# Low query parts and gate rows as 128-row operands padded with zeros, in a two-layer hybrid decoder step

## The chip, the cores and the metric

The kernel runs on one core of a Trainium2 chip. The metric is the device time of one execution in microseconds; the time of a kernel is the median of its runs.

## The reference

One step of a decoder with two trunk layers, for a prompt of 1024 tokens and a sample group of 8 x 4 tokens with 4096 cached ones each. A layer has a combined projection, four gated DeltaNet heads beside four differential attention heads, an output projection, a cross-attention and a gated MLP. What the change touches is the causal attention of the prompt (two 64-wide softmax maps per head) and the decay matrix of the DeltaNet:

```python
def diff_attention(q, k, v, q_pos, k_pos, lam):
    ...
        s = jnp.einsum('bqhd,bkhd->bhqk', qi, k).astype(jnp.float32) * scale
        s = jnp.where(k_pos[None, None, None, :] <= pi[None, None, :, None], s, -jnp.inf)
        p = jax.nn.softmax(s, axis=-1).reshape(B, H, 2, qb, Lk)
        a = p[:, :, 0] - lam * p[:, :, 1]
        return jnp.einsum('bhqk,bkhe->bqhe', a.astype(v.dtype), v)

def gated_delta_rule(q, k, v, g, beta, s0):
    ...
    gc = jnp.cumsum(chunks(g), axis=-1)
    decay = jnp.exp(jnp.where(lower, gc[..., :, None] - gc[..., None, :], -jnp.inf))
    kb = kc * bc[..., None]
    m = jnp.where(strict, jnp.einsum('nbhid,nbhjd->nbhij', kb, kc) * decay, 0.0)
    ...
```

Data are float32. The kernel multiplies at a shorter type with operands cut in two, a high part and a low part (the rest), and adds the products.

## The kernel before

Each layer runs as two interleaved streams: the prompt's (projection, DeltaNet beside attention, output projection, cross-attention, MLP) and the sample group's, which reads the cached keys and values page by page (tiles kn and vn) and is fed in between. A scheduler (the tile framework with its own model of the engines) fixes the order of all instructions on each engine when the program is built; on the chip each engine runs its own list in order and waits for semaphores.

TensorE holds one operand, the weights, which a load (LDWEIGHTS, shown as engine PEld) brings in, and streams the other. All of the TensorE's instructions are recorded at line 219, the helper that passes them on, so they are told apart by their tiles; a row "psA<-akT,aq" is a matmul into the accumulator psA that streams akT over the weights aq. A form 64\*128 means weights of 64 rows and 128 columns.

**Attention of the prompt** (`attn`, entered once a layer, after the projection). Queries and keys lie in DRAM as high and low parts (qksc), 64 dimensions for each of the two maps m of a head. `load` brings the keys of a head, tile akT, of 128 rows: for map 0 the high parts in rows 0 to 63 and the low parts in rows 64 to 127, for map 1 the other way round. `qload` brings the queries of two token tiles (256 tokens), tile aq, in three planes: planes 0 and 1 hold the high part of map 0 and 1 twice, in both halves of the rows, and plane 2 holds the low parts of both maps, map m in rows 64m to 64m+63. `scores` then makes, for a map and up to 512 keys, two matmuls into one accumulator: plane m against all 128 rows of akT (high query with high and low keys), and 64 rows of plane 2 against the 64 rows of akT with the high keys, placed at row 64m by tile_position. On the last piece a bfloat16 matmul of the mask cmn with an identity (identb) follows. DVE takes the maximum (mx), ScalarE the exponential (apr), and `values` transposes and multiplies with aV. There are 4 heads x 8 token tiles x 2 maps in a layer, in one piece of keys for the first four token tiles and two for the rest.

**DeltaNet.** `Gdn.rows` turns the cumulated gates of a chunk of 128 tokens into rows: tile hk, 64 rows, the high part from row 0, the low part from row 32, all else zero (zeroed by POOL). `decay` multiplies hk with the block pattern bma on POOL (tile R, L1170), and makes the exponent with three matmuls: R over weights of ones (oner, 64 rows), the block pattern bmbr over weights hk (64 rows), and the mask cmtb over identb (128 rows). `inputs` runs R over oner once more, alone. The eight chunks pass through `decay` in `gdn_first` (beside the end of the projection) and again in `gdn` (beside attention); the sample group passes once, in `gdn_samples`.

Queries, keys, pages and DeltaNet inputs all go out on SyncE's DMA queue (SP), in its order.

Of the kernel before, what the change touches and what calls it, by code (L numbers as in the profile page):

```python
# [9 lines left out]
F32 = mybir.dt.float32  # L10
F32R = mybir.dt.float32r
# [8 lines left out]
P = 128  # L20
# [165 lines left out]
def build(tc, a, out, depth=2):  # L186
# [12 lines left out]
    BC = (lambda z: z.bitcast(F32)) if XP[0] != '0' else (lambda z: z)  # L199
# [6 lines left out]
    QD = {'0': nc.gpsimd, '1': nc.scalar, '2': nc.sync}[XP[0]]  # L206
# [19 lines left out]
    v_, s_, g_, t_ = Tracked(nc.vector), nc.scalar, nc.gpsimd, Tracked(nc.tensor)  # L226
# [77 lines left out]
    def cload(pool_, key, rows=P, name=None, **kw):  # L304
        o, w = COFF[key]
        tl = pool_.tile([rows, w], F32, name=name or f"c_{key}", **kw)
        nc.sync.dma_start(tl, cst[0:rows, o:o + w])
        return tl
# [10 lines left out]
    ones = cp.tile([P, P], F32, name="ones")  # L319
# [5 lines left out]
    qksc = dp.tile([2, 2, 4, P, NP], F32, name="qksc")  # L325
# [205 lines left out]
    for t in range(9):  # L531
# [6 lines left out]
        for hf in range(2):  # L538
            ps = psA((P, 4, P))
# [6 lines left out]
    for k0 in range(0, KT, 3):  # L546
        m = min(3, KT - k0)
        raw = ip.tile([P, D], F32, tag="xt", bufs=5, name="raw")[:, 0:m * 264].rearrange("p (k c) -> p k c", c=264)
        nc.sync.dma_start(raw, a["w_in"][0][k0 * P:(k0 + m) * P, 2048:2312].rearrange("(k p) c -> p k c", p=P))
        for k in range(m):  # L550
            if (k0 + k) % 2 == 0:
                t = dk.tile([P, 1056], F32R, name="pre", tag="pg", bufs=PGB).rearrange("p (a b c) -> p a b c", a=2, b=2)
            hi, lo = t[:, (k0 + k) % 2, 0], t[:, (k0 + k) % 2, 1]
# [112 lines left out]
    for l in range(depth):  # L666
# [391 lines left out]
        class Gdn:  # L1058


            def __init__(self, gw, nh, nrow, tp, tag):
                self.gw, self.nh, self.nrow = gw, nh, nrow
                self.cm = gw.tile([P, P], BF16, name="cmtb")
                tmp = cload(tp, "cmt" if nh == 4 else "cmts", name="cmtmp", tag=tag, bufs=1)
                v_.tensor_copy(self.cm, tmp)
                self.utm = cload(gw, "ut" if nh == 4 else "uts")
                self.glm = ones if nh == 4 else cload(gw, "blks")
                self.oner = gw.tile([64, P], F32R, name="oner")
                v_.tensor_copy(self.oner, ones[0:64])
                self.bma = cload(gw, f"bma{nh}", rows=64)  # L1070
                tb_ = cload(gw, f"bmb{nh}", rows=64)
                self.bmb = gw.tile([64, nh, P], F32R, name="bmbr")
                v_.tensor_copy(self.bmb, bcast(tb_, 2, P))

            def small(self, nm, sh):
# [77 lines left out]
            def rows(self, f):  # L1153

                nh = self.nh
                tk = self.gw.tile([P, 2 * nh], F32, name="tk", tag="tk", bufs=2)
                g_.tensor_copy(tk[:, 0:nh], f["gc"])
                g_.tensor_copy(tk[:, nh:2 * nh], f["bias"])
                pt = psG()
                t_.transpose(pt[0:2 * nh, 0:P], tk, ident)  # L1160
                hk = self.gw.tile([64, P], F32R, name="hk", tag="hk", bufs=self.nrow)
                g_.memset(hk.bitcast(F32), 0.0)
                s_.copy(hk[0:2 * nh, :], pt[0:2 * nh, 0:P])
                v_.tensor_tensor(hk[32:32 + 2 * nh, :], pt[0:2 * nh, 0:P], hk[0:2 * nh, :].bitcast(F32), op=ALU.subtract)
                return hk

            def decay(self, wk, hk, bufs):
                nh = self.nh
                R = wk.tile([64, nh, P], F32R, name="R", tag="R", bufs=1)
                g_.tensor_tensor(R, bcast(hk.bitcast(F32), 1, nh), bcast(self.bma, 2, P), op=ALU.mult)  # L1170
                pe = self.ps()
                t_.matmul(pe, self.oner, R, start=True, stop=False)
                t_.matmul(pe, hk, self.bmb, start=False, stop=False)
                t_.matmul(pe, identb, bcast(self.cm, 1, nh), start=False, stop=True)
                E = self.work(wk, "E", bufs)
                s_.activation(E, pe, AF.Exp)
                return R, E
# [324 lines left out]
        def attn():  # L1502
            at = at_cm.__enter__()
# [9 lines left out]
            def load(h):  # L1513
# [6 lines left out]
                QX(14).dma_start(V, out["p_v"][l, 0, :, h, :].rearrange("(n p) e -> p n e", p=P))  # L1520
                return kT, V

            def qload(h, t2):
                qt = at.tile([P, 3, 2 * P], F32R, name="aq", tag="aq", bufs=2)
                cs = slice(t2 * 2 * P, (t2 + 1) * 2 * P)
                for k in range(2):
                    fetch(BC(qt[64 * k:64 * k + 64, 0:2, :]), qksc[0, 0, h, :, cs].rearrange("(m d) t -> d m t", m=2))
                QD.dma_start(BC(qt[:, 2, :]), qksc[0, 1, h, :, cs])
                return qt

            def scores(ld, qt, t):
                kT = ld[0]
                ts = slice((t % 2) * P, (t % 2 + 1) * P)
                nk = (t + 1) * P
                nch = (nk + 511) // 512
                pm, sums = [], []
                for m in range(2):
                    pss = []
                    mx = at.tile([P, 2], F32, name="mx", tag="mx", bufs=4)
                    lo = slice(64 * m, 64 * m + 64)  # L1540
                    for c in range(nch):
                        wdt = min(512, nk - c * 512)
                        ps = psA()
                        last = c == nch - 1
                        ks = slice(c * 512, c * 512 + wdt)
                        t_.matmul(ps[:, 0:wdt], qt[:, m, ts], kT[:, m, ks], start=True, stop=False)
                        t_.matmul(ps[:, 0:wdt], qt[lo, 2, ts], kT[lo, m, ks], start=False, stop=not last, tile_position=(64 * m, 0))
                        if last:
                            t_.matmul(ps[:, wdt - P:wdt], identb, cmn, start=False, stop=True)
                        v_.tensor_reduce(mx[:, c:c + 1], ps[:, 0:wdt], axis=AX.X, op=ALU.max)  # L1550
                        pss.append((ps, wdt))
                    nb = at.tile([P, 1], F32, name="nb2", tag="nb2", bufs=4)
                    if nch == 2:
                        v_.tensor_tensor(mx[:, 0:1], mx[:, 0:1], mx[:, 1:2], op=ALU.max)
                    v_.tensor_scalar(nb, mx[:, 0:1], -0.125, None, op0=ALU.mult)
                    l_ = apr1 if m else apr0
                    pr = l_.pop() if l_ else at.tile([P, NP], F32, name=f"apr{m}", tag=f"apr{m}", bufs=2 - m)
                    sm2 = at.tile([P, 2], F32, name="sm2", tag="sm2", bufs=4)
                    for c, (ps, wdt) in enumerate(pss):
                        s_.activation(pr[:, c * 512:c * 512 + wdt], ps[:, 0:wdt], AF.Exp, scale=0.125, bias=nb, accum_out=sm2[:, c:c + 1])  # L1560
                    if nch == 2:
                        v_.tensor_tensor(sm2[:, 0:1], sm2[:, 0:1], sm2[:, 1:2], op=ALU.add)
                    pm.append(pr)
                    sums.append(sm2)
                    yield nk * 2 / 2400.0 + 0.1
# [51 lines left out]
            ld = load(0)  # L1617
            seq = [(h, t) for h in range(4) for t in (range(7, -1, -1) if XP[18][h] == "d" else range(8))]
            qt = qload(0, seq[0][1] // 2)
            for i, (h, t) in enumerate(seq):  # L1620
# [12 lines left out]
                if i % 2:  # L1633
                    qt = qn
# [792 lines left out]
```

## Time and profile before

| what | us |
|---|---|
| median of three plain runs | 4163.96 (4162.37 to 4166.68) |
| the profiled execution, its own time | 4172.92 |
| its span in the trace | 4171.1 |
| PE busy | 3863.1 (93%) |
| PEld busy | 2988.1 (72%) |
| DVE busy | 2256.6 (54%) |
| ACT (ScalarE) busy | 1311.7 (31%) |
| POOL busy | 1174.7 (28%) |

Busy times overlap, and PE's are drawn out by matmuls whose end is modelled; the distance from one start to the next tells more than the duration of one. The two attention stages lie at about 605 to 930 us and 2625 to 2945 us of the span. A row of the timeline gives start, length, engine, line, operation, out<-in, shapes and how many instructions it merges, and in brackets the idle time ahead of it with what ended it; "issue" is idle time for which the profile shows no releaser.

### The profile page before, as it was taken

To read this page: it belongs to the slowest core of one execution; us is meant where nothing else is said; L and a number is where in the kernel's file an instruction comes from. 1 tells how busy PE (TensorE), PEld (TensorE's weight loads), DVE (VectorE), ACT (ScalarE), POOL (GpSimd) and SP (SyncE) were. 2 spreads that over 40 slices of the span, in tenths; PEclk is the share of its full clock that TensorE was granted. 3 is DMA by queue.
4 is the path that set the end of the run, shared out by engine and by line. 5 is a ranking of instruction groups with operands and counts; after the bars stand their busy time and mean duration, and the time that the engine had idled before them with its cause. 6 is when DMAs were issued, how large, how long until landed. Compare 5 with 4: busy or idle time off the path is not lost. (4 is left out here: it accounts for less than half of the span.)

```text
span 4171.1 us, 72714 instructions
## 1 busy us (share of the span) xinstructions
PE 3863.1 (93%) x25178; PEld 2988.1 (72%) x25178; DVE 2256.6 (54%) x3907; ACT 1311.7 (31%) x2823; POOL 1174.7 (28%) x1125
## 2 busy tenths in 40 slices
PE   6899979979899999999979998889799999999999
PEld 5789866756667766776769987567566766677667
DVE  7355556863676544343367466577465734443334
ACT  4333424441442212321243253333334312222111
POOL 6452412222322212112246242132231311212211
PEclk8999979999999999999989999799899999999999
DMA  5464587647545543447427565764754455444751
GB/s 176 130 192 147 164 225 192 188 131 214 153 127 163 176 145 110 144 152 227 135 83 219 154 173 182 203 199 130 224 170 125 141 168 154 122 132 133 222 169 61
DMA packets 626469, 673.14 MB, mean 161 GB/s; under 512 B 76875, under 2 KB 444438, under 8 KB 626102
## 3 DMA queue, kind: packets, MB, share of 16 engines
q1 hardware_dynamic: 581475, 638.35, 51.4%
q10 hardware_dynamic: 42963, 25.81, 2.0%
q8 instruction: 200, 3.28, 0.3%
q0 software_dynamic: 1664, 4.33, 0.3%
q14 instruction: 167, 1.37, 0.1%
HBM read 588.12 MB, written 80.17 MB: 160 GB/s over the span
## 5 line engine op out<-in xcount | busy, mean ns | idle before, releaser
L377 POOL TENSOR_TENSOR wlo<-raw,whi 128x1024 fp32r<-128x1024 f32 (+1 forms) x308 | 531.0, 1736 | 1454.5 <-ACT whi L376 1349.5
L219 PE MATMUL psA<-hh,whi 128*128 128x512 f32 (+1 forms) x2096 | 794.1, 379 | 52.5 <-ACT whi L376 22.0
L219 PE MATMUL psA<-hl,whi 128*128 128x512 f32 (+1 forms) x2096 | 790.2, 377 | 4.4 <-DVE hl L219 2.7
L219 PE MATMUL psA<-hh,wlo 128*128 128x512 f32 (+1 forms) x2096 | 788.2, 376 | 0.0
L219 PEld LDWEIGHTS psA<-hh,whi 128*128 128x128 f32 x2096 | 399.7, 191 | 167.2 <-issue 34.0
L376 ACT CAST whi<-raw 128x1024 fp32r<-128x1024 f32 (+1 forms) x308 | 237.7, 781 | 766.0 <-PE psA L219 405.4
L219 PEld LDWEIGHTS psA<-hh,wlo 128*128 128x128 f32 x2096 | 399.2, 190 | 84.9 <-issue 27.2
L219 PEld LDWEIGHTS psA<-hl,whi 128*128 128x128 f32 x2096 | 400.9, 191 | 77.6 <-issue 14.9
L219 DVE STREAM_TRANSPOSE T<-kn 128x1024 f32<-128x1024 f32 x256 | 308.8, 1227 | 119.3 <-PE psB L219 109.6
L219 DVE TENSOR_TENSOR x<-x,psA 128x512 f32<-128x512 f32 x296 | 201.0, 683 | 248.0 <-PE psA L219 239.0
L219 DVE TENSOR_SCALAR fcv<-fraw,pvf 128x1024 f32<-128x1024 f32 x44 | 94.3, 2142 | 352.4 <-ACT fraw L2037 330.1
L219 PE MATMUL psG<-hh,whi 128*128 128x512 f32 x560 | 227.2, 406 | 0.9 <-ACT whi L376 0.9
L219 PE MATMUL psG<-hl,whi 128*128 128x512 f32 x560 | 225.6, 403 | 1.0 <-DVE hl L219 1.0
L219 PE MATMUL psG<-hh,wlo 128*128 128x512 f32 x560 | 223.8, 400 | 0.0
L219 PE MATMUL psA<-hi,hh 128*128 128x256 f32 (+1 forms) x720 | 205.4, 286 | 5.2 <-DVE cxn L219 4.1
L219 PE MATMUL psA<-ah,whi 128*128 128x512 f32 x484 | 195.7, 406 | 10.7 <-ACT whi L376 10.7
L219 PE MATMUL psA<-lo,hh 128*128 128x256 f32 (+1 forms) x720 | 203.8, 283 | 0.6 <-POOL lo L391 0.6
L219 PE MATMUL psA<-hi,hl 128*128 128x256 f32 (+1 forms) x720 | 204.4, 284 | 0.0
L219 PE MATMUL psA<-al,whi 128*128 128x512 f32 x484 | 195.0, 404 | 0.0
L219 PE MATMUL psA<-ah,wlo 128*128 128x512 f32 x484 | 193.9, 402 | 0.0
L219 PE MATMUL psA<-akT,aq 128*128 128x512 f32 (+7 forms) x384 | 154.5, 452 | 30.6 <-DMA aq<-qksc 30.6
L219 PE MATMUL psC<-vn,pT 128*32 128x512 f32 x1024 | 171.6, 626 | 7.8 <-DMA vn<-in_cache_v_dram 7.8
(516 smaller groups left out, 7331.0 us busy)
## 6 DMA issues: line engine op xcount, KB each, us to landing
kn<-in_cache_k_dram SPq DMA_DIRECT2D x512, 256.0 KB
vn<-in_cache_v_dram SPq DMA_DIRECT2D x1024, 128.0 KB
raw<-in_w_gate_dram SPq DMA_DIRECT2D x44, 512.0 KB
raw<-in_w_up_dram SPq DMA_DIRECT2D x44, 512.0 KB
raw<-in_w_down_dram SPq DMA_DIRECT2D x44, 512.0 KB
sw<-in_w_down_dram SPq DMA_DIRECT2D x44, 512.0 KB
sw<-in_w_gate_dram SPq DMA_DIRECT2D x48, 384.0 KB
sw<-in_w_up_dram SPq DMA_DIRECT2D x48, 384.0 KB
```

The source lines that it names most:

```text
L219: r = f(*args, **kw)
L376: s_.copy(hi, raw)
L377: g_.tensor_tensor(lo, raw, hi.bitcast(F32), op=ALU.subtract)
```

## The change

The low queries get tiles of their own. Two tiles zq of 128 rows with a plane for each map are made once per layer; the half of each plane that belongs to the other map is zeroed once by POOL, and `qload`, which takes the two tiles in turn, writes the low part of map m into rows 64m to 64m+63 of plane m, in two DMAs of 64 rows instead of one of 128. The low matmul then uses all 128 rows of zq against all 128 rows of akT. The tile aq keeps two planes. In the DeltaNet oner, bma, bmbr, hk and R get 128 rows; rows 64 to 127 are zero in bma, bmb (their constants are zero there) and hk.

```diff
-                self.oner = gw.tile([64, P], F32R, name="oner")
-                v_.tensor_copy(self.oner, ones[0:64])
-                self.bma = cload(gw, f"bma{nh}", rows=64)
-                tb_ = cload(gw, f"bmb{nh}", rows=64)
-                self.bmb = gw.tile([64, nh, P], F32R, name="bmbr")
+                self.oner = gw.tile([P, P], F32R, name="oner")
+                v_.tensor_copy(self.oner, ones)
+                self.bma = cload(gw, f"bma{nh}")
+                tb_ = cload(gw, f"bmb{nh}")
+                self.bmb = gw.tile([P, nh, P], F32R, name="bmbr")
...
-                hk = self.gw.tile([64, P], F32R, name="hk", tag="hk", bufs=self.nrow)
+                hk = self.gw.tile([P, P], F32R, name="hk", tag="hk", bufs=self.nrow)
...
-                R = wk.tile([64, nh, P], F32R, name="R", tag="R", bufs=1)
+                R = wk.tile([P, nh, P], F32R, name="R", tag="R", bufs=1)
...
+            zq = [at.tile([P, 2, 2 * P], F32R, name=f"zq{i}") for i in range(2)]
+            for z in zq:
+                g_.memset(z[64:128, 0].bitcast(F32), 0.0)
+                g_.memset(z[0:64, 1].bitcast(F32), 0.0)
+            nq = [0]
+
             def qload(h, t2):
-                qt = at.tile([P, 3, 2 * P], F32R, name="aq", tag="aq", bufs=2)
+                qt = at.tile([P, 2, 2 * P], F32R, name="aq", tag="aq", bufs=2)
+                z = zq[nq[0] % 2]
+                nq[0] += 1
                 cs = slice(t2 * 2 * P, (t2 + 1) * 2 * P)
                 for k in range(2):
                     fetch(BC(qt[64 * k:64 * k + 64, 0:2, :]), qksc[0, 0, h, :, cs].rearrange("(m d) t -> d m t", m=2))
-                QD.dma_start(BC(qt[:, 2, :]), qksc[0, 1, h, :, cs])
-                return qt
-
-            def scores(ld, qt, t):
+                for m in range(2):
+                    QD.dma_start(BC(z[64 * m:64 * m + 64, m, :]), qksc[0, 1, h, 64 * m:64 * m + 64, cs])
+                return qt, z
+
+            def scores(ld, qz, t):
...
-                        t_.matmul(ps[:, 0:wdt], qt[lo, 2, ts], kT[lo, m, ks], start=False, stop=not last, tile_position=(64 * m, 0))
+                        t_.matmul(ps[:, 0:wdt], z[:, m, ts], kT[:, m, ks], start=False, stop=not last)
```

The scheduler makes a new order within the two attention stages; before, between and behind them PE's order is the one of before. On PE, early in the attention of the first layer (in_ are DeltaNet inputs, kc the sample group's, apr and aT attention's probabilities; a number in a name tells tiles of one kind apart):

```order
-L219 MATMUL psG<-c_ident,in_8384 128x128 x4
-L219 MATMUL psG<-c_ident,in_8386 128x128 x4
+L219 MATMUL psG<-c_ident,in_8392 128x128 x4
 L219 MATMUL psA<-c_ident,apr_8339 128x128
+L219 MATMUL psG<-c_ident,in_8394 128x128 x4
+L219 MATMUL psA<-aV,aT 128x128
+L219 MATMUL psA<-akT,aq 128x384
+L219 MATMUL psA<-akT,zq_8346 128x384
+L219 LDWEIGHTS identb
+L219 MATMUL psA<-cmn,identb 128x128
```

The pair of a high and a low matmul stays together, now over aq and zq, and the transposes of the DeltaNet inputs and the value matmul are woven in otherwise. On POOL, at the end of the first layer's projection, before:

```order
L1162 MEMSET hk 64x128
L1308 MEMSET U 128x512
L1170 TENSOR_TENSOR R<-hk,c_bma_5679 64x512
L1308 MEMSET U 128x512
L1157 COPY tk<-gc 128x1
```

and now:

```order
L1162 MEMSET hk 128x128
L1526 MEMSET zq_8345 64x256
L1527 MEMSET zq_8345 64x256
L1526 MEMSET zq_8346 64x256
L1527 MEMSET zq_8346 64x256
L1308 MEMSET U 128x512
L1170 TENSOR_TENSOR R<-hk,c_bma_5679 128x512
L1308 MEMSET U 128x512
L1157 COPY tk<-gc 128x1
```

The four zeroing instructions stand ahead of the first multiplication of gate rows. On SP, at the first query loads of the first layer:

```order
 L1520 DMA aV<-out_p_v_dram 128x8x128
 L359 DMA aq<-qksc 64x2x256 x2
-L1528 DMA aq<-qksc 128x256
+L1538 DMA zq_8345<-qksc 64x256 x2
 L359 DMA aq<-qksc 64x2x256 x2
-L1528 DMA aq<-qksc 128x256
+L1538 DMA zq_8346<-qksc 64x256 x2
```

Where one low load stood, two stand now.

## Rows read from the trace of the kernel before

**Rows 1.** The page, busy us, share of the span and instructions.

```profile
PE 3863.1 (93%) x25178; PEld 2988.1 (72%) x25178; DVE 2256.6 (54%) x3907; ACT 1311.7 (31%) x2823; POOL 1174.7 (28%) x1125
```

**Rows 2.** Stretches of time: length, busy us by engine, granted clock, DMA share, GB/s.

```profile
605.00:930.00 325.00, 289.74 (x2117) 213.79 (x2118) 231.38 (x552) 135.61 (x469) 83.68 (x90) 0.93 0.62 173
2625.00:2945.00 320.00, 294.64 (x2054) 217.34 (x2054) 226.57 (x536) 128.49 (x453) 76.44 (x85) 0.90 0.62 173
...
740.00:800.00 60.00, 54.64 (x439) 43.97 (x437) 49.16 (x105) 25.63 (x91) 17.29 (x17) 0.97 0.70 205
800.00:860.00 60.00, 56.35 (x450) 43.82 (x450) 48.63 (x111) 25.44 (x91) 11.68 (x12) 1.00 0.47 135
```

**Rows 3.** Timeline of the weight loads in attention, 824.7 to 828.7 us.

```profile
824.76 0.19 PEld L219 LDWEIGHTS psA<-akT,aq 128*128 128x128 f32 x1
825.19 0.18 PEld L219 LDWEIGHTS psA<-akT,aq 64*128 64x128 f32 x1 [0.24 <-issue]
825.62 0.97 PEld L219 LDWEIGHTS psG<-G,NTl 128*128 128x128 f32 x8 [0.25 <-issue]
...
827.80 0.10 PEld L219 LDWEIGHTS <-identb 128*128 128x128 bf16 x1 [0.24 <-issue]
827.81 0.20 PEld L219 LDWEIGHTS psA<-akT,aq 128*128 128x128 f32 x1
```

**Rows 4.** Timeline of PE in dense stretches of 128-row matmuls, 512 and 256 columns.

```profile
1500.86 0.39 PE L219 MATMUL psA<-hh,whi 128*128 128x512 f32 x1
...
1502.97 0.40 PE L219 MATMUL psA<-hh,whi 128*128 128x512 f32 x1
...
215.36 0.28 PE L219 MATMUL psA<-hi,hh 128*128 128x256 f32 x1
...
215.95 0.28 PE L219 MATMUL psA<-hi,hh 128*128 128x256 f32 x1
```

**Rows 5.** Timeline of the weight loads around a decay matrix, 423.9 to 425.5 us.

```profile
423.86 0.19 PEld L219 LDWEIGHTS psA<-hl,whi 128*128 128x128 f32 x1
424.02 0.19 PEld L219 LDWEIGHTS psA<-hh,wlo 128*128 128x128 f32 x1
424.43 0.18 PEld L219 LDWEIGHTS psG<-R,oner 64*128 64x128 f32 x1 [0.22 <-issue]
424.54 0.19 PEld L219 LDWEIGHTS psG<-bmbr,hk 64*128 64x128 f32 x1
425.08 0.10 PEld L219 LDWEIGHTS <-identb 128*128 128x128 bf16 x1 [0.35 <-issue]
```

**Rows 6.** By tile: count, ns min/median/max, first and last start; last row by form.

```profile
L219 PEld LDWEIGHTS psA<-akT,aq x384: 182/186/338, 605.5 to 2926.9; 128*128 128x128 f32 x184, 64*128 64x128 f32 x8
L219 PE MATMUL psA<-akT,aq x384: 217/474/796, 605.5 to 2926.9; 128*128 128x512 f32 x96, 128*128 128x384 f32 x32, 128*128 128x256 f32 x30, 128*128 128x128 f32 x26
...
L219 PE MATMUL psG<-R,oner x52: 323/496/792, 424.4 to 2906.4; 64*128 64x512 f32 x48, 64*128 64x128 f32 x4
...
L219 PE MATMUL psG<-bmbr,hk x34: 383/393/413, 424.8 to 2900.7; 64*128 64x512 f32 x32, 64*128 64x128 f32 x2
...
L219 PE MATMUL psA<-akT,aq 64*128 64x128 f32 x32 | 10.5, 329 | 0.0
```

**Rows 7.** Timeline of the weight loads of a 256-wide pair and its mask.

```profile
649.55 0.50 PEld L219 LDWEIGHTS psA<-akT,aq 128*128 128x128 f32 x2 [0.20 <-issue]
650.18 0.10 PEld L219 LDWEIGHTS <-identb 128*128 128x128 bf16 x1
```

**Rows 8.** POOL by form: count, busy us, mean ns, idle time ahead and releasers.

```profile
L1170 POOL TENSOR_TENSOR R<-hk,c_bma 64x512 fp32r<-64x512 f32 x32 | 37.3, 1165 | 38.0 <-PE psG L219 21.2 <-DVE hk L219 10.6 <-DMA vn<-in_cache_v_dram 2.6
...
L1605 POOL TENSOR_TENSOR oraw<-oraw,ass 128x512 f32<-128x512 f32 x16 | 16.6, 1039 | 87.8 <-ACT ass L468 87.8
```

**Rows 9.** PE's first score in the timeline; the low query loads by tile.

```profile
605.49 1.19 PE L219 MATMUL psA<-akT,aq 128*128 128x128 f32 x4 [13.51 <-DMA aq<-qksc]
...
L1528 SPq DMA_DIRECT2D aq<-qksc x32: 327/586/1242, 597.8 to 2886.4; - x32
```

More of the change, by code (lines that the diff above doesn't have):

```diff
@@ L1527, in qload @@
                     fetch(BC(qt[64 * k:64 * k + 64, 0:2, :]), qksc[0, 0, h, :, cs].rearrange("(m d) t -> d m t", m=2))
-                QD.dma_start(BC(qt[:, 2, :]), qksc[0, 1, h, :, cs])
-                return qt
-            def scores(ld, qt, t):
+                for m in range(2):
+                    QD.dma_start(BC(z[64 * m:64 * m + 64, m, :]), qksc[0, 1, h, 64 * m:64 * m + 64, cs])
+                return qt, z
+            def scores(ld, qz, t):
                 kT = ld[0]
+                qt, z = qz
                 ts = slice((t % 2) * P, (t % 2 + 1) * P)
@@ L1539, in scores @@
                     mx = at.tile([P, 2], F32, name="mx", tag="mx", bufs=4)
-                    lo = slice(64 * m, 64 * m + 64)
                     for c in range(nch):
```

## The prediction, made before the changed kernel ran

> **What bounds the kernel now.** I read the page first: TensorE (PE) is busy for 93% of the span [rows 1], so a stage is shortened by shortening what PE does in it, as long as nothing else is as full there. Then I read the order of the instructions before and after the change. Outside the two attention stages (one in each layer) PE runs the same instructions in the same order, so the stage to look at is attention, 605 to 930 us and 2625 to 2945 us. There PE is busy 289.7 of 325 and 294.6 of 320 us, so it stands still for 35.3 and 25.4 us, while VectorE (DVE) works 71% of the time, ScalarE 41%, GpSimd (POOL) 25% [rows 2]. PE is the bound, with a tenth of slack.
>
> Next I looked at what PE does in one score: the view of its weight loads (PEld), at the full clock [rows 3]. The load of a high part starts at 824.76; the load of the 64-row low part only at 825.19, after the load engine stood idle for 0.24 us "for issue"; the next load, of 128 rows again, at 825.62, after another 0.25 us. So each of the two matmuls holds PE for 0.43 us. Compare a stretch in which all operands have 128 rows: matmuls of the same 512 columns start every 0.234 us (1500.86 to 1502.97, nine of them) [rows 4], and their loads of 0.19 us are hidden under the matmul before. The difference, 0.20 us, is about the 0.18 us that a load lasts: a load that changes the number of rows, from 128 to 64 or back, waits until the running matmul is through, and then lies bare.
>
> That it is the change of height, and not 64 rows as such, is seen in the gate rows of the DeltaNet [rows 5]. The load for the multiplied gate rows (64 rows) starts 0.41 us after a 128-row load, where the loads ahead came every 0.16. The next load, again of 64 rows, follows 0.11 us later, long before the matmul between them can be through: it is hidden. The next one, of 128 rows, waits 0.35 us. Two changes, two bare loads.
>
> The Trainium skill speaks on both sides of this. "TensorEngine Tiling (Array Packing)", Key Properties, says that changing the tiling mode drains the TensorE; the trace agrees, at 0.20 us a change [rows 3, 4]. "TensorE: Matmul & The Clock Gate", Part 3, says that a load overlaps running matmuls only when its row group differs. By that a 128-row load would never hide; it is rival C below, and the dense stretch speaks against it [rows 4].
>
> **The change part by part.**
>
> *Scores.* 384 matmuls of this kind are 192 pairs of a high and a low one; 32 pairs are 128 columns wide, 160 are wider [rows 6]. A 512-wide pair takes 0.86 us now and 2 x 0.234 = 0.47 dense: 0.39 saved. A 256-wide one takes 0.63 us, from 649.55 to 650.18 [rows 7], and dense 2 x 0.118 (215.36 to 215.95, five matmuls) [rows 4]: 0.39 again, so the saving doesn't depend on the width as long as the load is the same, and I take it for 384 too. For 128 columns no dense row exists; I take half a dense 256 (0.059) off each matmul of the 256 pair now, 0.63 - 0.12 = 0.51, and leave the dense one at 0.118 each: 0.28. Together 160 x 0.39 + 32 x 0.28 = 71.4 us.
> In 128 of the pairs the mask matmul (identb) follows the low one. Now its short load and that of the next high part go out together (827.80 and 827.81) [rows 3], so it costs next to nothing; later it costs its own 128 columns, by the same half of 0.118: 128 x 0.06 = 7.7 us back. Scores: 63.7 us.
>
> *Gate rows.* There are 52 runs of 64-row matmuls: 34 of two (gate rows, then block rows) and 18 alone [rows 6]. From the load ahead of such a run (424.02) to the one behind it (425.08) go 1.06 us [rows 5]; dense it would be 0.16 + 2 x 0.234 = 0.63. So 34 x 0.43 + 18 x 0.39 = 21.6 us. Sixteen of the double runs lie in the projection before attention, where PE has no slack either.
>
> *Clock.* The sum so far is 85.3 us, at the full clock. In the two windows the granted clock is 0.93 and 0.90 [rows 2], so PE is at the lower of its two levels (1.2 instead of 2.4 GHz) for 14 to 20% of the time. There a load lasts up to 338 ns instead of 182 [rows 6], and a bare one costs that much more: some 78 us x 17% x 0.86 = 11. PE has 96 us less to do.
>
> *What POOL and the queues get.* The multiplication of the gate rows goes from 64 to 128 partitions; POOL takes 1165 ns for 64 rows x 512 and 1039 for 128 x 512 of another kind [rows 8], so I count nothing. Four zeroing instructions a layer stand ahead of the first multiplication in POOL's order and wait until the projection's memory is free; at no more than 1.2 us each (the multiplication's own price) that is 4.7 us at most, just where PE waits 13.5 us for its first queries [rows 9]: nothing, 5 us a layer if that cover were gone. The low queries come in two DMAs of 64 rows instead of one of 128, on SyncE's queue: 32 issues more at 586 ns [rows 9], 19 us of a queue that waits for others much of the time; the bounds are 0 and 19, and I take 0, because the bytes are the same and the loads go out two tiles ahead. The casts of the constants to 128 rows happen four times in all and are nothing.
>
> *What is late next.* The same DVE work, 458 us in the two windows, in 78 + 11 = 89 us less is 82% instead of 71%. From 740 to 860 us DVE is already at 81% (97.8 of 120), and PE still busy for 111 of 120 us [rows 2]: a DVE this full doesn't stop PE by itself. But PE now waits for results (scores' maxima, the copies of transposes) that used to come during its bare loads. I let a quarter of the gain go there: 96 - 24 = 72 us. The ends are everything kept (96, or 104 if the mask matmul stays free) and the case of rival B.
>
> The profiled execution took 4172.9 us (span 4171.1 and 1.8 around it), 9.0 over the median of the three plain runs. Against it the sum is 4172.9 - 72 = 4100.9; against the median, which is what will be compared, 4164.0 - 72 = **4092 us**.
>
> **The rivals.**
>
> *B: another engine takes over.* PE gets its 96 us, but in the chains score - maximum - exponential - transpose - value and DeltaNet step after step it now mostly waits for DVE and ScalarE; two thirds are given back. For: DVE at 71 to 81%, few PSUM banks between PE and the rest, and a new order within the stage that was not made for this. Against: the waits of PE there are few, 61 us in 645, and spread. Some 15 to 50 us remain, say 30: 4134.
>
> *C: the padded load stays bare.* If what holds the load is that it needs rows which the running matmul uses, then 128 rows after 128 are no better, and nothing is gained: 4164. That is what the second rule of the Trainium skill above would give. Against it stand the dense stretch, where loads of 128 rows hide under matmuls of 128 rows throughout [rows 4], and the second gate load, which hides on the rows of the first [rows 5].
>
> *D: slower, by the queue.* The two halves of the low queries are written into two fixed buffers, and each half waits on SyncE until PE has read it last; behind it stand page loads of the decoding group, DeltaNet inputs and states. If a wait there holds the queue so that PE starves, each of 32 loads can cost more than it brings. The gain of 72 us is gone from 72 / 32 = 2.3 us of PE's time per load; at 4 us it would be 4164 - 72 + 128 = 4220. Against: the combined tile waits for the same readers now, and the first queries are the only ones for which PE waited long [rows 9].
>
> **How the numbers follow.** The forecast (50 to 104 us gained, 4060 to 4114) gets 0.62, because every term of it is read from rows in which the same loads hide or don't. B gets 0.22, C 0.08, D 0.08. A change within 0.2% (8.3 us) can't be told from none by a measurement of this kernel. Faster: 0.62 + 0.22 = 0.84; same: C, 0.08; slower: D, 0.08. The range goes from all of the gain kept (4060) into B as far as about 20 us gained (4144): 0.62 and about 0.18 of B's 0.22.
>
> **What would show it right or wrong.** In the weight loads of the changed kernel the low part (zq, now 128 rows) should start about 0.1 to 0.2 us after the high one's, without 0.24 us of idle time for issue, and the pair of 512 columns should take 0.47 us. The gate runs should lose their gaps likewise. The attention stages should be shorter by 30 to 40 us each, the rest unchanged but for some 7 us before attention. DVE's share there should rise to about 80%. If the loads hide and the stage is not shorter, look at PE's waits for DVE and ScalarE (B); if the gaps of 0.24 us are still there, C is right; if PE waits for DMAs of zq, page or DeltaNet tiles in the middle of the stage, D. The forecast is wrong altogether if the bare load came from something that the padding doesn't touch, such as the kind of data of the two parts.

## The result, and the profile after

The changed kernel takes 4131.64 us (median of 4 runs, 4126.24 to 4135.6) against 4163.16 for the kernel before beside it: a ratio of 0.9927, 95% interval 0.9913 to 0.994, some 30 us less. A second series (e10 below) gave 0.9937 (0.9921 to 0.9953). The direction is as forecast, but the forecast was 72 us. What came is the time of rival B, 4134, and the time lies in the stated range only because that range reached into B. The profiled execution took 4129.26 us (span 4127.5).

The page after, as in [rows 1]:

```profile
PE 3786.4 (92%) x25178; PEld 2967.8 (72%) x25178; DVE 2233.1 (54%) x3905; ACT 1314.8 (32%) x2825; POOL 1181.8 (29%) x1133
```

The view by tile of the changed kernel shows the low part as planned, 192 matmuls over 128 rows, and the zeroing (count, ns min/median/max, first and last start; after the semicolon the forms):

```profile
L219 PE MATMUL psA<-akT,zq x192: 220/390/696, 606.0 to 2891.9; 128*128 128x512 f32 x96, 128*128 128x128 f32 x32, 128*128 128x256 f32 x32, 128*128 128x384 f32 x32
L1538 SPq DMA_DIRECT2D zq<-qksc x64: 454/554/1166, 597.7 to 2858.2; - x64
L1526 POOL MEMSET zq<- x4: 307/307/307, 585.6 to 2577.4; 64x256 f32 x4
```

The timeline of its weight loads, as in [rows 3] and [rows 5]:

```profile
824.01 0.19 PEld L219 LDWEIGHTS psA<-akT,aq 128*128 128x128 f32 x1
824.12 0.19 PEld L219 LDWEIGHTS psA<-akT,zq 128*128 128x128 f32 x1
824.59 0.10 PEld L219 LDWEIGHTS <-identb 128*128 128x128 bf16 x1 [0.28 <-issue]
824.59 0.20 PEld L219 LDWEIGHTS psA<-akT,aq 128*128 128x128 f32 x1
824.71 0.19 PEld L219 LDWEIGHTS psA<-akT,zq 128*128 128x128 f32 x1
824.95 1.09 PEld L219 LDWEIGHTS psG<-U,X 128*128 128x128 f32 x8
...
827.79 0.19 PEld L219 LDWEIGHTS psG<-R,oner 128*128 128x128 f32 x1 [0.28 <-DVE U L219]
827.90 0.19 PEld L219 LDWEIGHTS psG<-bmbr,hk 128*128 128x128 f32 x1
828.36 0.10 PEld L219 LDWEIGHTS <-identb 128*128 128x128 bf16 x1 [0.27 <-issue]
```

The low load (zq) starts 0.11 us after the high one (aq), and the load behind a pair without a mask 0.24 us after that: the gaps of 0.24 us for issue between the parts are gone. Only the load of the bfloat16 identity still has one, 0.26 to 0.28 us.

From the first score to the last output of a head (DVE's od), the two attention stages last 312.1 and 307.9 us, before 325.5 and 323.8: 29 us less. Ahead of attention less than 2 us were gained. Between and behind the stages the profiled execution is 5 and 9 us shorter, but that of e1 below, whose matmuls have the old height, is 8 and 9 us shorter there too: this is the spread of executions (that of the kernel before took 9 us more than its median). So the gain is where it was looked for, and the question is why it is half.

### The profile page after: what moved, and what is told of

Read it like the earlier page. It is cut to its first block, busy times and chain, and to the rows that moved or that the text cites. A ratio compares the mean times of both kernels' runs of the same rounds, so it can differ in the third digit from the quotient of the medians.

```text
span 4127.5 us, 72754 instructions
## 1 busy us (share of the span) xinstructions
PE 3786.4 (92%) x25178; PEld 2967.8 (72%) x25178; DVE 2233.1 (54%) x3905; ACT 1314.8 (32%) x2825; POOL 1181.8 (29%) x1133
## 5 line engine op out<-in xcount | busy, mean ns | idle before, releaser
L219 PE MATMUL psA<-ah,whi 128*128 128x512 f32 x484 | 195.3, 405 | 10.1 <-ACT whi L376 10.1
L1570 ACT ACTIVATE apr<-psA,nb 128x512 f32<-128x512 f32 (+2 forms) x192 | 110.1, 581 | 159.0 <-DVE nb L219 152.1
```

Source lines behind the costliest of these rows:

```text
L219: r = f(*args, **kw)
```

## The experiments

All ratios are to the kernel before on the same chip. Where the two heights are compared, "64 rows" means the changed kernel's tiles, DMAs and zeros with the low and gate matmuls over 64 of the rows.

**The height alone: e1.**

```diff
-                        t_.matmul(ps[:, 0:wdt], z[:, m, ts], kT[:, m, ks], start=False, stop=not last)
+                        lo = slice(64 * m, 64 * m + 64)
+                        t_.matmul(ps[:, 0:wdt], z[lo, m, ts], kT[lo, m, ks], start=False, stop=not last, tile_position=(64 * m, 0))
...
-                t_.matmul(pe, self.oner, R, start=True, stop=False)
-                t_.matmul(pe, hk, self.bmb, start=False, stop=False)
+                t_.matmul(pe, self.oner[0:64], R[0:64], start=True, stop=False)
+                t_.matmul(pe, hk[0:64], self.bmb[0:64], start=False, stop=False)
```

> The changed kernel with its tiles, its DMAs, its zeroing and, on every engine, its order of instructions, but the matmuls over zq, oner and hk use only the 64 rows that are not zero, as before. Theory 1 (the height of the operand is what saves, and the rest of the change is neutral): the time of the kernel before, ratio 0.998 to 1.002 (4155 to 4171 us), attention stages of 325 us each, gaps of 0.24 us ahead of the low loads again. Theory 2 (the padding saves more than the result shows, and the new order with its additional loads costs 15 to 30 us): slower than before, ratio 1.004 to 1.007 (4179 to 4193 us). Theory 3 (the gain comes from the order, not from the height): the time of the changed kernel, ratio 0.993.

Measured: 1.0013 (1.0000 to 1.0025). Every engine has the order of the changed kernel, so its queue, zeroing, POOL work and new order cost about 5 us together, and the height of the operands alone brings 32 to 36 us (0.9937 and 0.9927 against 1.0013). The same stretch of PE's timeline in e1, and then in the changed kernel, gives the price of one:

```profile
832.98 0.48 PE L219 MATMUL psA<-akT,aq 128*128 128x512 f32 x1
833.39 0.49 PE L219 MATMUL psA<-akT,zq 64*128 64x512 f32 x1
833.81 0.23 PE L219 MATMUL psA<-cmn,identb 128*128 128x128 bf16 x1
833.88 1.11 PE L219 MATMUL psG<-S,in 128*128 128x128 f32 x8
```

```profile
825.99 0.47 PE L219 MATMUL psA<-akT,aq 128*128 128x512 f32 x1
826.30 0.39 PE L219 MATMUL psA<-akT,zq 128*128 128x512 f32 x1
826.53 0.23 PE L219 MATMUL psA<-cmn,identb 128*128 128x128 bf16 x1
826.60 1.11 PE L219 MATMUL psG<-S,in 128*128 128x128 f32 x8
```

From the high matmul to what follows the mask: 0.90 us in e1, 0.61 in the changed kernel, 0.29 saved (forecast 0.39 - 0.06 = 0.33). Read likewise, a pair without a mask saves 0.40 and a 128-wide one with its mask 0.225 (0.39 and 0.22). So the scores' term is 64 x 0.40 + 96 x 0.29 + 32 x 0.225 = 60.6 us where 63.7 was forecast. A double gate run is read at the loads: in e1

```profile
834.91 0.18 PEld L219 LDWEIGHTS psG<-R,oner 64*128 64x128 f32 x1
835.02 0.19 PEld L219 LDWEIGHTS psG<-bmbr,hk 64*128 64x128 f32 x1
835.57 0.10 PEld L219 LDWEIGHTS <-identb 128*128 128x128 bf16 x1 [0.36 <-issue]
```

it takes 0.66 us from R to the identity, after 0.57 (827.79 to 828.36, above): 0.09 less there, with the bare load ahead of it (0.20) 0.29, not 0.43. The mask's load behind it stays bare. With the forecast's 0.39 for a run alone, 34 x 0.29 + 18 x 0.39 = 17 us, forecast 21.6.

**The two halves apart: e2 (scores over 128 rows, gates over 64) and e3 (the other way round)**, each with one half of e1's diff; in e2 the last of three matmuls is

```diff
-                t_.matmul(pr, self.oner, R, start=True, stop=True)
+                t_.matmul(pr, self.oner[0:64], R[0:64], start=True, stop=True)
```

> The changed kernel in its order, with 128 rows in the score matmuls only; the gate rows (oner, R, hk, bmbr) are multiplied over 64 rows as before. If PE's time is kept in proportion, scores have three quarters of the bare loads (192 pairs against 52 runs of gate rows): ratio 0.9945 (4140 us) where the changed kernel has 0.9927. If the gate rows lie on the path that the waits set in attention and in the projection, they bring more than their share: 0.997. If they bring nothing: 0.9927.

> The complement: the changed kernel in its order, 128 rows in the gate rows only, the low queries over 64 rows. Proportional: about a quarter of the gain, 8 us, ratio 0.998 (4155 us). If the gate rows bring nothing, the ratio is that of the kernel with 64 rows everywhere. With the other two this also shows whether the two parts add up: gain of both = gain of scores + gain of gates within 5 us, or less than the sum if a common limit (another engine, the DMAs) cuts it.

Measured: e2 0.9944 (0.9927 to 0.996), e3 1.0000 (0.9987 to 1.0013). Against e1 the scores bring 29 us of their 60.6, the gates 5 of their 17, and the two add up to what both bring together. Each interval reaches 5 to 7 us to either side, so the gates' 5 us are not clear of nothing. A common floor, an engine that is full at some point, would have cut only the second of them; within that spread there is no sign of one.

**The mask as float32: e4.**

```diff
-    identb = cp.tile([P, P], BF16, name="identb")
+    identb = cp.tile([P, P], F32R, name="identb")
```

> The changed kernel with the mask operands (identb, cmn, cmtb) in float32r in place of bfloat16, so that all matmuls of a score and of a decay matrix have the same type; results are the same. Theory: in the changed kernel the short load of identb still starts only when the low matmul is through (0.27 us idle for issue), now because of its type; with float32r it hides, 162 times about 0.2 us = 32 us of PE, of which half is kept as in the change itself: ratio 0.989 (4115 us). Rival: the bare load of identb costs little, since the next high load goes out with it, and a float32r mask streams longer than a bfloat16 one: ratio 0.992 to 0.996.

Measured: 0.9935 (0.992 to 0.995), as the changed kernel. In the timeline of e4's weight loads the gap for issue is gone:

```profile
822.39 0.19 PEld L219 LDWEIGHTS psA<-akT,aq 128*128 128x128 f32 x1
822.50 0.19 PEld L219 LDWEIGHTS psA<-akT,zq 128*128 128x128 f32 x1
822.74 0.19 PEld L219 LDWEIGHTS psA<-cmn,identb 128*128 128x128 f32 x1
822.98 0.19 PEld L219 LDWEIGHTS psA<-akT,aq 128*128 128x128 f32 x1
```

but from one high load to the next go 0.59 us, as with the bare bfloat16 load (824.01 to 824.59, above: 0.58). It is the same at a double gate run: at the first of them in the projection (R at 422.50 us in e4, at 423.48 in the changed kernel) the identity's load follows R by 0.39 us in e4 and by 0.61 in the changed kernel, but the load behind the identity by 0.62 in both. There was nothing to gain.

**VectorE as the bound: e8 and e9**, without the subtraction of the second map, over 128 and 64 rows.

```diff
-                    v_.scalar_tensor_tensor(pm[0][:, 0:nk], pm[1][:, 0:nk], cc, pm[0][:, 0:nk], op0=ALU.mult, op1=ALU.add)
+                    pass
```

> The changed kernel without the step that takes the second map's probabilities, times lambda, off the first map's: 64 instructions of VectorE over up to 1024 columns, some 45 us of its work, all within the attention stages. (Attention's result is then that of the first map alone.) Theory DVE (with PE's bare loads gone, VectorE sets much of the pace): 20 us or more faster than the changed kernel, ratio 0.988 or less. Theory DMA: under 10 us faster, 0.990 to 0.993.

> The same step left out, with matmuls over 64 rows. Theory DVE: here PE is the bound, so leaving the step out brings little (ratio 0.997 to 1.001), and between this kernel and the one above the padding brings 50 us or more, nearer to the 53 us that PE's busy time fell by in the two windows. Theory DMA or order: this step matters equally little in both, and the difference stays at 30 to 40 us.

Measured: e8 0.9932 (0.9916 to 0.9948), e9 1.0020 (1.0009 to 1.003): the pair keeps 0.9% of the time, where the whole change kept 0.8 to 0.9. VectorE works 389 us in the two stages of e8 and 445 in those of the changed kernel, and still the kernel is not faster. In the stages themselves the pair gains 36 us where e1 and the changed kernel differ by 27, but the projection of the second layer got another order in e8 and lost 9. VectorE is one of those that PE waits for, not the bound.

**More buffers for the sample group's states: e6 and e7**, since PE's waits for these states had grown.

```diff
-                    S0 = gs.tile([P, 2, 4, P], F32, name="S0", tag="S0", bufs=1)
+                    S0 = gs.tile([P, 4, P], F32, name="S0", tag="S0", bufs=3)
```

> The changed kernel, with the sample group's DeltaNet states loaded one batch at a time into three buffers (6 KB a partition) in place of two batches at a time into one (4 KB), so that a load need not wait until PE has read the last; the order within the attention stages is made anew. PE's waits for these states grew from 7.8 to 14.9 us when the low operands went from 64 to 128 rows in the same order. Theory DMA (what the padding gave back went into waits for transfers that start too late): these waits fall under 5 us and the kernel is 8 to 12 us faster than the changed one, ratio to before 0.990 to 0.991. Theory DVE, or chains of short dependences on all engines: another wait takes their place, ratio 0.992 to 0.995.

> The same with matmuls over the 64 rows that are not zero (order all but equal to the one above: some 200 of 15,000 rows of PE moved). Theory DMA: the padding brings more with these loads out of the way, 45 us or more between this kernel and the one above, against 36 us between the kernels without this edit (ratios 1.0013 and 0.9927). Otherwise again 30 to 40 us, and this kernel at 0.999 to 1.003.

Measured: e6 0.9965 (0.9953 to 0.9976), e7 1.0019 (1.001 to 1.0029), so 0.5% apart. The stages gain 27.4 us from 64 to 128 rows (20 and 8 by layer), in all as without the buffers; the waits for the states stay in e6 (3.0 and 7.1 us). The edit reaches only the loads for the state products; the loads for the state updates keep their two buffers. It also changes the order of the second layer's projection (9 us longer in both), so that neither can be set beside the changed kernel, only beside the other.

**An earlier start: e11**, with e10, the changed kernel once more, beside it. The first queries are loaded ahead of the first keys, and these come in two pieces.

```diff
+                for c0, c1 in ((0, 256), (256, NP)) if h == 0 else ((0, NP),):
...
-            ld = load(0)
             seq = [(h, t) for h in range(4) for t in (range(7, -1, -1) if XP[18][h] == "d" else range(8))]
             qt = qload(0, seq[0][1] // 2)
+            ld = load(0)
```

> The changed kernel once more, on the same chip and beside the same runs of the kernel before as e11_early, so that the two are compared without the spread between chips. Expected by every theory: 0.990 to 0.995 of the kernel before (0.9927 in the first result).

> The changed kernel, and in addition the first queries of each layer are loaded ahead of the first keys, and the first head's keys are loaded in two pieces of 256 and 768 columns, so that the first scores need less data. TensorE's order outside the attention stages is unchanged. It touches the one long wait of attention: the two opening waits of TensorE for the first queries are 15.1 and 17.2 us in the changed kernel. Theory (half of the saved time is given back in many short waits inside the stage, and the opening wait is apart from these): the opening waits fall by 4 to 6 us each and the stages by as much, 8 to 12 us less than the changed kernel, ratio 0.990 to 0.991 if that is 0.9927 or so again. Rival (what ends the opening is the total of the bytes in the queue, or DeltaNet's work beside it ends the stage anyway): the opening waits fall, but the time stays within 4 us of the changed kernel, 0.992 to 0.994.

Measured: e10 0.9937, e11 0.9948 (0.9932 to 0.9965). PE's first score, in e10 and in e11:

```profile
605.74 1.19 PE L219 MATMUL psA<-akT,aq 128*128 128x128 f32 x4 [14.30 <-DMA zq<-qksc]
```

```profile
600.73 0.45 PE L219 MATMUL psA<-akT,aq 128*128 128x128 f32 x1 [9.83 <-DMA akT<-qksc]
```

The opening waits fell by 4.5 and 4.1 us, as expected, and the time did not follow: the theory's 8 to 12 us are not there, and the interval takes in the rival's 0.992 to 0.994. In layer 1, laid beside e10, the start was given back within the first 45 us of the stage. This is what made me ask where in the stage the gain arises.

**Instruction beside instruction.** e1 and the changed kernel run the same list on PE, so the same instruction can be looked up in both timelines. For e1 (first fence) and the changed kernel:

```profile
603.59 1.19 PE L219 MATMUL psA<-akT,aq 128*128 128x128 f32 x4 [14.41 <-DMA zq<-qksc]
...
766.89 1.16 PE L219 MATMUL psG<-U,X 128*128 128x128 f32 x8 [1.78 <-DVE S L219]
...
928.65 1.92 PE L219 MATMUL psC<-vn,pT 128*32 128x512 f32 x4
```

```profile
604.91 1.20 PE L219 MATMUL psA<-akT,aq 128*128 128x128 f32 x4 [15.12 <-DMA zq<-qksc]
...
763.90 1.16 PE L219 MATMUL psG<-U,X 128*128 128x128 f32 x8 [3.42 <-DVE S L219]
...
916.86 1.92 PE L219 MATMUL psC<-vn,pT 128*32 128x512 f32 x4
```

From the first score to the U,X of the second row go 163.30 us in e1 and 158.99 in the changed kernel: 4.3 gained in 163. From there to the end go 161.76 and 152.96: 8.8 gained. The wait ahead of that U,X shows how a gain is lost: 1.78 us became 3.42. The trace leads it back to a load. This S is a state of the sample group; VectorE adds to it behind GpSimd's multiplication, and that had waited for the DMA (e1, then the changed kernel):

```profile
765.07 1.05 POOL L1494 TENSOR_TENSOR S<-S,egm 128x512 f32<-128x512 f32 x1 [4.16 <-DMA S<-in_state_gdn_dram]
```

```profile
762.08 1.05 POOL L1494 TENSOR_TENSOR S<-S,egm 128x512 f32<-128x512 f32 x1 [4.06 <-DMA S<-in_state_gdn_dram]
```

Cut at the same place in both layers (part 1 is the stage up to about 165 us after the first score, part 2 the rest), in us gained from 64 to 128 rows, layer 1 and layer 2:

| pair | part 1 | part 2 | kept in part 1, in part 2 |
|---|---|---|---|
| e1, changed kernel | 4.3, 1.7 | 8.8, 12.1 | 16%, 60% |
| e1, e10 | 2.3, 3.5 | 7.8, 13.0 | 16%, 60% |
| e13, states left out | 3.8, 9.5 | 3.6, 14.5 | 36%, 52% |
| e12, pages halved | 13.5, 8.4 | 8.0, 9.1 | 53%, 55% |

What is kept is measured against what is freed by the prices above. Part 1 holds 50 pairs in each layer (16 without a mask, 24 wide and 10 narrow with one) and 4 + 5 gate runs: 15.6 + 3.1 = 18.7 us; part 2 holds 46 (16, 24, 6) and 4 + 4: 17.4. For the other pairs the freed time is scaled with the number of score pairs in the part. Two profiled executions of the same kernel (rows one and two) differ by up to 2 us in such a cell. The spread beyond that pair is larger: e2 and e4, cut in the same way and set beside e1, have 7.2, 3.1 and 5.1, 6.5 in part 1 and 9.5, 10.1 and 2.1, 10.3 in part 2. All of these are read against one profiled execution of e1, the fastest of its twelve and 11 us under their median, so the gains may be a few us too small.

So the two parts hold nearly the same score and gate matmuls and differ in what they keep. The stretches of time differ as well (length, then busy us of PE, PEld, DVE, ACT and POOL, granted clock, DMA share, GB/s); e1, then the changed kernel:

```profile
603.50:768.00 164.50, 145.42 (x999) 101.53 (x1000) 108.89 (x279) 63.52 (x222) 50.27 (x60) 0.92 0.72 197
768.00:928.80 160.80, 144.28 (x1125) 110.39 (x1125) 122.77 (x275) 70.80 (x245) 31.12 (x28) 0.98 0.49 145
2610.30:2779.00 168.70, 146.12 (x1030) 102.71 (x1030) 111.42 (x285) 65.90 (x229) 47.44 (x60) 0.90 0.75 203
2779.00:2932.00 153.00, 144.67 (x1036) 109.33 (x1036) 108.38 (x257) 63.46 (x225) 26.78 (x26) 0.96 0.48 144
```

```profile
605.00:765.00 160.00, 131.59 (x999) 101.54 (x1000) 107.47 (x279) 63.62 (x222) 50.77 (x60) 0.90 0.74 202
765.00:917.00 152.00, 131.71 (x1125) 110.21 (x1125) 121.13 (x276) 70.98 (x245) 31.71 (x28) 0.96 0.52 153
2601.00:2766.00 165.00, 135.21 (x1030) 103.66 (x1030) 110.17 (x285) 65.98 (x229) 45.59 (x58) 0.88 0.76 206
2766.00:2909.00 143.00, 128.63 (x1036) 105.83 (x1036) 106.65 (x257) 63.96 (x225) 28.15 (x27) 0.97 0.54 157
```

PE lost 11 to 14 us of work in each part 1, but by the table the part became only 2 to 4 us shorter. VectorE is less busy in part 1 (67% in the changed kernel) than in part 2 (80% and 75%). The DMA engines are the other way: 0.72 to 0.76 of the time at about 200 GB/s in part 1, half in part 2. In part 1 runs the sample group's DeltaNet with its states, and beside those states 76 loads of cached pages come in (layer 1).

Some of the loss in part 1 is the clock's. The sixteen matmuls aV,aT behind the U,X above last 1.79 us to the next start in e1 (767.89 to 769.68, granted clock 1.00) and 3.05 us in e10 (767.73 to 770.78, granted 0.56, so some 2.7 us at 1.2 instead of 2.4 GHz): nearly half of the time at the lower level is lost. In part 1 of both layers the granted clock fell by 0.02 from e1 to the changed kernel, which is about 6 us more at the lower level in each. With the clock of e1 the two would have gained, by this estimate, some 11 us instead of 6, three tenths of what is freed.

**What takes the gain in part 1: e13 and e12**, each over 128 and over 64 rows. e13 leaves out most of the sample group's state work, e12 half of the page loads.

```diff
-                for hb in range(4):
+                for hb in range(1):
...
-            for b in range(NB):
+            for b in range(1):
```

```diff
                 hf = i % 2
+                if hf:
+                    halves[i] = halves[i - 1]
+                    return
```

> The changed kernel, without three quarters of the sample group's DeltaNet state products (one of four state tiles is loaded and multiplied) and without seven of the eight state updates (one state is updated and written in all eight places); the sample group's DeltaNet output and states are therefore not the reference's. Compared with e13_states_64. Theory S (in the first half of the stage the sample group's DeltaNet, a chain of loads and products on a few buffers, goes at its own pace and takes the gain): without it the two stages gain 40 to 48 us in all from 64 to 128 rows, not 27, and the first half of each about 10 instead of 2 to 4. Theory M (the supply of data): also more, by the 3.7 MB less in the queue per stage, but no more than e12. Rival G (many short waits that any part of the stage has): the pair's difference stays at 24 to 30 us. Time by itself: below the changed kernel, since work is left out, by 20 to 60 us.

> The same with the low queries and gate rows multiplied over 64 rows, in practically the same order on TensorE: the other half of the pair. The difference of the two is what is asked: 40 to 48 us in the stages by theory S, 24 to 30 by rival G.

> The changed kernel with half of the loads of cached pages left out (the second half of each page group uses the data of the first), so that the sample group's attention is not the reference's. Compared with e12_pages_64, whose TensorE order is the same. Theory M (in the first half of the stage PE waits for the supply of data through SyncE's queue, of which the pages are the largest part): the stages gain 38 to 48 us from 64 to 128 rows. Theory S and rival G: 24 to 30 us as before, 2 to 5 us in the first half of each stage.

> The same with 64 rows, the same order on TensorE: the other half of the pair. The difference of the two is what is asked: 38 to 48 us in the stages by theory M, 24 to 30 by S and G.

Measured: e13 0.9883 (0.9859 to 0.9907) over 128 rows and 0.9959 (0.9942 to 0.9976) over 64, 31 us apart, of which 31.6 in the stages. e12 0.9578 (0.9555 to 0.9601) and 0.9683 (0.9655 to 0.971), 43 us apart, of which 38.8 in the stages. The first is below what theory S wanted (40 to 48), the second at the lower edge of theory M's range (38 to 48). The table says it by part: with the pages halved part 1 keeps as much as part 2.

By the table e13 gained as much in layer 2's part 1 (9.5) as e12 (8.4). The clock tells the two apart. Layer 2 of e13, part 1 and part 2, over 64 rows and then over 128:

```profile
2616.00:2786.80 170.80, 152.89 (x995) 113.99 (x996) 112.76 (x285) 65.14 (x226) 34.93 (x40) 0.86 0.68 188
2786.80:2946.00 159.20, 144.39 (x958) 103.94 (x957) 107.71 (x254) 70.14 (x244) 28.41 (x26) 0.87 0.46 137
```

```profile
2606.20:2767.50 161.30, 133.27 (x994) 108.97 (x995) 111.02 (x285) 64.76 (x225) 34.92 (x40) 0.89 0.72 199
2767.50:2912.20 144.70, 119.03 (x958) 96.72 (x957) 104.39 (x254) 70.21 (x244) 28.74 (x26) 0.95 0.50 149
```

The execution over 64 rows ran some 39 us more at the lower level than the one over 128, which by the price above is 18 of the 24 us gained in that layer. In e12 the clock differs in layer 1 (0.92 and 0.95 below, some 4 of the 13.5 us) and is 0.95 in both in layer 2's part 1. With the clock taken off, an estimate, part 1 gains some 17 us in e12 over both layers, 11 in the changed kernel and 6 in e13. So theory S finds no support, and theory M is ahead by less than the table shows.

The stretches of layer 1's part 1 in e12, over 64 rows and then over 128:

```profile
579.00:740.00 161.00, 146.66 (x1062) 105.10 (x1066) 114.44 (x285) 64.35 (x226) 50.43 (x61) 0.92 0.66 177
```

```profile
579.00:740.00 161.00, 140.00 (x1153) 110.76 (x1153) 126.44 (x311) 69.78 (x242) 54.38 (x65) 0.95 0.71 191
```

Over 64 rows the loads now come at 177 GB/s, not 197, and so there is room to go faster: over 128 rows PE gets through 1153 matmuls in the same 161 us. PE's longest waits for DMAs in layer 2's part 1, but for the opening one, show the same thing from the other end, in e1 and then in the changed kernel:

```profile
PE psG L219 <- DMA S<-in_state_gdn_dram: 4.6, 3, 3.5
```

```profile
PE psG L219 <- DMA S<-in_state_gdn_dram: 9.0, 3, 5.2
PE psA L219 <- DMA aq<-qksc: 2.0, 1, 2.0
```

So do GpSimd's waits for the states that it updates, in the changed kernel and then in e12 over 128 rows (the same instruction, which e12's edit moves by three lines; count, busy time and mean ns, then the idle time ahead and what ended it):

```profile
L1494 POOL TENSOR_TENSOR S<-S,egm 128x512 f32<-128x512 f32 x16 | 17.4, 1094 | 46.9 <-DMA S<-in_state_gdn_dram 40.3 <-DVE mx L219 3.4 <-ACT egm L1472 1.7
```

```profile
L1497 POOL TENSOR_TENSOR S<-S,egm 128x512 f32<-128x512 f32 x16 | 16.7, 1048 | 31.0 <-DMA S<-in_state_gdn_dram 13.5 <-DVE mx L219 4.6 <-DVE sm L219 3.2
```

In e1 they are 35.4 us: with the pages halved, the states come sooner.

So the supply of data in part 1 is the likeliest reason for the loss there, but it is not shown. The differences of whole runs (43 and 32 to 36 us) are too close for their intervals to part them, and by the stages' total e8 and e9 (36 us) would speak for VectorE as e12 (38.8) does for the data, so the verdict rests on the parts and on single profiled executions. And halving the pages takes away both bytes and issues on SyncE's queue, so which of the two it is stays open, as does why part 2 keeps only six tenths.

## Why the prediction was wrong

- **The mechanism** held: a load that changes its height lies bare, a 128-row load behind a 128-row matmul hides. Rival C, which followed from the Trainium skill's "TensorE: Matmul & The Clock Gate", Part 3, is ruled out: loads of 128 rows follow one another at 0.11 us, and e1 shows that the height alone makes the difference.
- **The scores' term**, 63.7 us, measured 60.6. The mask's cost, which was charged at 0.06, is there.
- **The gate rows' term**, 21.6, came out at 17, 0.14 us a double run less. The forecast took the wait of the identity's load as saved. The load stays bare, as it is bfloat16; but with a float32 identity, whose load hides, the load behind it comes no sooner (e4). So the likely reason is the mask's own columns, which the forecast charged in the scores and not here.
- **The clock's term**, 11 us, was too large. The forecast spread the 17% over all bare loads, but by the granted clock only 18 of the 192 low matmuls of the kernel before lie at the lower level. There a 384-wide pair with its mask saves 0.39 us (2617.27 to 2618.54 in e1, 2607.01 to 2607.89 in the changed kernel) and 0.29 at the full clock: some 3 us in all, an estimate. Without the term some 78 us are freed, not 96.
- **"A quarter of the gain goes there" is the step that failed.** Of 78 us freed 32 to 36 were kept, less than half; 24 us given back were forecast, 42 to 46 were. The forecast saw only DVE as what could be late next, and took 740 to 860 us, of which three quarters are part 2, as its witness that a busy engine doesn't stop PE. It did not use the DMA share, which stands at 0.70 in the first half of that very stretch [rows 2] and which a table of the stages by thirds would have shown at 0.78 and 0.76 in their first thirds, and it took the two stages as one piece of which PE is the bound throughout. What the runs show in its place is that part 1, with the DMA engines at 0.72 to 0.76, kept a sixth of what was freed and part 2 six tenths; that the supply of data is the cause is likely and open.
- **Rival B** gave the time (4134) for a partly wrong reason: not DVE and ScalarE taking over (DVE is at 73% and 70% in the two stages of the changed kernel, and e8, with 56 us less of its work, is no faster), but a part in which more things than PE set the pace.
- **POOL and the queues** at nothing: right. Multiplying gate rows takes 1171 ns (1165 in [rows 8]), zeroing 0.307 us each instead of the bound of 1.2, and PE's opening waits are 15.1 and 17.2 us in the changed kernel and 14.4 and 15.6 in e1, with 13.5 [rows 9] and 17.1 before. New order and loads together cost 5 us (e1). Rival D's time is out, but its sign, waits for DeltaNet tiles in the middle of the stage, is there: PE's waits for the states are 4.6 us before, 7.8 in e1 and 14.9 in the changed kernel.
- **What was to be seen**: loads 0.11 us apart, yes; a pair of 512 columns in 0.47 us, 0.54 (822.25 to 822.79) for the first two starts but 0.40 saved with what follows; stages 30 to 40 us shorter, no, 13 and 16; 7 us ahead of attention, no, under 2; DVE at 80%, no.

## What to carry to other kernels

Here a weight load that changes the number of rows cost about its own length (0.20 us), and padding the small operand with zeros to the height of its neighbours took that away at no price in the tensor engine's columns. Before the freed time is put down as gained, cut the stage into parts and look in each for the second most loaded resource, the DMA share included: here two parts with nearly the same score and gate matmuls kept about a sixth and six tenths. Two kernels with the same order can be laid instruction beside instruction, which shows where a gain arises and where it is lost far more sharply than sums of waits; set the granted clock of both beside it, since by the estimate above a different clock made up 18 of 24 us in one case here (e13).

## What the runs showed of the hardware that was not expected

A bfloat16 load behind a float32 matmul of the same height is bare for 0.26 to 0.28 us, and a float32 load in its place is not (e4). The bare load costs nothing here: the load behind comes at the same time with either type, behind a pair with its 128-column mask (0.58 and 0.59 us) and behind a double gate run with its 512-column mask (0.62 in both). The zero rows cost PE nothing that can be seen: 128-row low matmuls of 512 columns follow their high ones by 0.31 us, 64-row ones by 0.41 to 0.43.
